# One written order for four engines up to the first values, a logarithm norm of x, and first weights loaded in quarters

## The chip, the cores and the metric

The kernel runs on one core of one Trainium2 chip. The metric is the device time of one execution in microseconds (us), lower is better. The median of three runs of the kernel before is 1539.29 us (1538.88 to 1541.18). One further execution was taken with the hardware profiler; its own time is 1536.77 us, and its span, from the first to the last instruction, 1535.1 us.

## The reference

Two layers of an encoder, 512 tokens by 1024 features, all in f32. The change touches only the head of layer 0: the first RMS norm and the products that take its result.

```python
def rms_norm(x, gain):
    xf = x.astype(jnp.float32)
    y = xf * lax.rsqrt(jnp.mean(xf * xf, axis=-1, keepdims=True) + EPS)
    return (y * gain.astype(jnp.float32)).astype(x.dtype)

def hgrn2_mixer(x, w_in, o_norm, w_out, lb):      # x is rms_norm(h, pre_mix_norm[0])
    proj = x @ w_in                                # 1024 -> 5 * 1024
    q, f_fw, f_bw, inp, gate = jnp.split(proj, ...)
    v = heads(inp)                                 # the "values"
    ...                                            # gated linear recurrence, both directions
    return (o * jax.nn.silu(gate)) @ w_out

def rope_angles(positions, dim):                   # needed only in layer 1
    inv = 1.0 / (ROPE_BASE ** (jnp.arange(0, dim, 2, dtype=jnp.float32) / dim))
    ang = positions.astype(jnp.float32)[..., None] * inv
    return jnp.cos(ang), jnp.sin(ang)

for i in range(DEPTH):
    a = rms_norm(h, pre_mix_norm[i])
    m = hgrn2_mixer(a, ...) if i % 2 == 0 else mla_mixer(a, positions, ...)
    h = h + rms_norm(m, post_mix_norm[i])
    f = squared_relu_mlp(rms_norm(h, pre_mlp_norm[i]), w_mlp_in[i], w_mlp_out[i])
    h = h + rms_norm(f, post_mlp_norm[i])
    h = h + rms_norm(jax.nn.sigmoid(h @ w_ple_gate[i]) * (p[i] @ w_ple_proj[i]), ple_norm[i])
```

## The kernel before

Every large product runs as three matmuls: each operand is split into a rounded part `hi` (type fp32r) and a rest `lo`, and hi·hi, hi·lo and lo·hi are summed in PSUM (`mm3`). A product's weights arrive by DMA in a raw tile (2048 columns, two buffers). The class `Weights` holds a written list of jobs; for each, ScalarE (ACT) makes `whi` by a copy to fp32r (L109) and VectorE (DVE) makes `wlo` by a subtraction. In the traces and orders below these are the tiles `whi`, `wlo` and `raw`.

Activations lie transposed: features on the 128 partitions, tokens on columns. So at the start x (four blocks of 128 tokens, tiles `x`, t = 0 to 3) is normed by row, transposed on TensorE (PE) in 128 by 128 pieces, and split with its gain into `ah` (ACT, L346) and `al` (DVE, L347); one `ah` tile holds two of the eight feature blocks k. `normed(ts)` does that for a list of token blocks: sum of squares, `rsqrt` (an integer guess and refinement in a dozen tiny DVE instructions), the scaling of x (L525), the transposes, the splits.

`first_values` multiplies the normed blocks with the first half of the value weights (four jobs "v", two raw tiles). Its results gather in the PSUM tiles `nm` (t=0), `sm` (t=1) and two `mm` tiles (t=2, 3): 24 matmuls of 512 columns for each t, 96 in all. After them comes the loop over the heads, which begins with the projections f, b, q and g of head 0, 24 matmuls each.

In the source the lower bound `lb` of the gates (tiles `mx`, `es`, `tot`) and the tables of the rotary angles come after that. The angles are a chain of small instructions on GpSimd (POOL), from the positions (`pos`, `posf`) through 15 rounds of `k`, `ang` (L577 to L586); then ACT takes a sine, an absolute value and a sine again (`sin_t`, `ang`, `cos_t`, L590 to L593). These need another table of functions than the rest of the kernel, so a table load stands ahead of them and one behind. Nothing reads `sin_t` and `cos_t` before layer 1. When they are done, the pool `start`, with x in it, is given back, and its memory is filled with x again (tile `H`, L602).

What sets the order: all loads of weights and of x are issued by SyncE (SP), in program order, on one DMA queue. On the computing engines the framework's scheduler lays the order down when the program is built, from a timeline of its own. Each engine then takes its instructions strictly in that order. Where the kernel wants its own order it wraps an engine in `Ordered` and calls `keep(True)`: instructions issued through the wrapper are then tied to each other in the order of the source. Before the change the head ties only PE's warm-up transposes.

Of the kernel before, what the change touches and what calls it, by code (L numbers as in the profile page):

```python
# [26 lines left out]
ALU = mybir.AluOpType  # L27
# [27 lines left out]
class Weights:  # L55

    def __init__(self, nc, pool, lo, ahead, raw_bufs, split_bufs):
        self.nc, self.pool, self.lo, self.ahead = nc, pool, lo, ahead  # L60
# [35 lines left out]
    def _split(self, i):  # L96
        nc = self.nc
        while self.n_split <= i and self.n_split < len(self.jobs):
            key, raw, lo_eng, copies, prep = self.jobs[self.n_split]
            if self.raws[raw][2] not in self.kinds:  # L100
                return
            self._load(raw)
            t = self.raws[raw][1][0]
            if prep:
                prep(t)
            hi = self.pool.tile([P, 1024], F32R, tag="whi", bufs=self.split_bufs, name=f"whi{self.n_split}")
            lo = self.pool.tile([P, 1024], F32R, tag="wlo", bufs=self.split_bufs, name=f"wlo{self.n_split}")
            for dst, src in copies:
                nc.scalar.copy(dst(hi), src(t))  # L109
# [26 lines left out]
class Ordered:  # L136


    def __init__(self, tc, eng):
        self.tc, self.eng, self.on, self.last = tc, eng, False, None  # L140

    def keep(self, on):
        self.on, self.last = on, None

    def __getattr__(self, name):
        def issue(*args, **kw):
            i = getattr(self.eng, name)(*args, **kw)  # L147
            if self.on:
                if self.last is not None:
                    self.tc.add_manual_dep(i.ins, self.last.ins.name, mybir.DependencyInfo(  # L150
                        mybir.DependencyClass.NoSync, mybir.DependencyReason.DATA), reason="in order")
                self.last = i
# [9 lines left out]
def trunk(  # L162
# [27 lines left out]
    def mm_tile():  # L190
        return T(pm, [P, S], "mm", 5)
# [5 lines left out]
        return T(pm, [P, S], "nm", 1)  # L197


    W = Weights(nc, wp, VN, ahead=4, raw_bufs=2, split_bufs=5)  # L200

    def plan_pair(keys, src, r0, c0, c1, lo=None):

# [286 lines left out]
    nc.sync.dma_start(pos, positions.rearrange("o (t p) -> p (o t)", p=P))  # L490
    nc.sync.dma_start(frq, freq.to_broadcast([P, 32]))

    warm = mm_tile()
    gps = mm_tile()
    PE.keep(True)
# [4 lines left out]
    PE.keep(False)  # L500
    V.tensor_copy(gains, gps[:, :ROWS])

    act = act_tiles()[0]
    ss, rx = T(sp, [P, NT], "ss"), T(sp, [P, NT], "rx")

    def normed(ts):

        a, n = ts[0], len(ts)
        hf = slice(a * P, (a + n) * P)
        for t in ts:  # L510
            v = ss[:, t : t + 1]
            if t < 3:
                junk = T(sp, [P, D], "junk", 2)
                A.activation(junk, xt[t], AF.Square, accum_out=v)
                V.tensor_scalar(v, v, 1.0 / D, EPS, op0=ALU.mult, op1=ALU.add)
            else:
                st, mv = T(sp, [P, 2, 6], "bn_st", 2), T(sp, [P, 2], "bn_mv", 2)
                for c in range(2):
                    V.bn_stats(st[:, c], xt[t][:, c * S : c * S + S])
                V.bn_aggr(mv, st)  # L520
                V.scalar_tensor_tensor(v, mv[:, 0:1], mv[:, 0:1], mv[:, 1:2], op0=ALU.mult, op1=ALU.add)
                V.tensor_scalar(v, v, EPS, None, op0=ALU.add)
        rsqrt(ss[:, a : a + n], rx[:, a : a + n])
        for t in ts:
            V.tensor_scalar(xt[t], xt[t], rx[:, t : t + 1], None, op0=ALU.mult)  # L525
        m = 2
        for k in range(0, NB, m):
            ps = mm_tile()
            for j in range(m):
                for t in range(n):  # L530
                    c = (n * j + t) * P
                    PE.transpose(ps[:, c : c + P], xt[a + t][:, (k + j) * P : (k + j + 1) * P], ident)
            for j in range(m):
                hi, lo = act[k + j]
                split(ps[:, j * n * P : (j + 1) * n * P], hi[:, hf], lo[:, hf], gain("pre_mix", k + j))
# [976 lines left out]
```

## Time and profile before

| | us |
|---|---|
| median of three runs | 1539.29 |
| the profiled execution | 1536.77 |
| its span | 1535.1 |
| PE busy in the span | 1499.4 (98%) |
| DVE busy | 1016.4 (66%) |
| ACT busy | 771.4 (50%) |
| POOL busy | 188.6 (12%) |
| mean granted clock of TensorE, share of full speed | 0.996 |

Times of rows count from the first instruction. "Busy" is the time in which an engine has an instruction under way; matmuls overlap, so a busy PE may still be slowed by its clock. A row of a timeline gives start, duration, engine, line and operation, and in brackets how long the engine had been idle and what ended that.

### The profile page before, as it was taken

Reading aid. Unit: us, or ns where it says so; the run is one execution under the profiler, and the core shown is the slowest. Engines: PE = TensorE matmul, PEld = TensorE weight load, DVE = VectorE, ACT = ScalarE, POOL = GpSimd, SP = SyncE. Lnnn points to the kernel's source line nnn. Section 1 sums busy time; section 2 is a strip of 40 time slices with the busy share of each in tenths; the row PEclk is TensorE's granted clock in tenths of the full one; section 3 lists DMA queues with packets and bytes.
Section 4 is the critical chain, followed back from the end, with each engine's and each line's share of the span. In section 5 each row is a group of like instructions: output and inputs, shape, how many; then the busy total and the mean of one; then the engine's idle time right before and its main releaser. Section 6 shows DMA issues by size and latency. Waiting matters only on the chain.

```text
span 1535.1 us, 19274 instructions
## 1 busy us (share of the span) xinstructions
PE 1499.4 (98%) x7379; PEld 1252.5 (82%) x7379; DVE 1016.4 (66%) x1842; ACT 771.4 (50%) x1319; POOL 188.6 (12%) x208
## 2 busy tenths in 40 slices
PE   8999999999999999999999999999999999999997
PEld 6888888889888787888887888888788887878885
DVE  6688578655675949456787784378464747677476
ACT  6555455356555454434645564466355645445332
POOL 4233132200000000000113331432000000000000
PEclk9999999999999999999999999999999999999999
DMA  5622332137151322314321111220552150604221
GB/s 168 204 57 82 83 83 83 42 121 245 47 178 42 141 79 75 117 57 136 118 88 30 42 56 56 59 81 30 185 186 82 36 184 1 220 0 137 85 81 55
DMA packets 109950, 147.86 MB, mean 96 GB/s; under 512 B 4781, under 2 KB 78114, under 8 KB 109602
## 3 DMA queue, kind: packets, MB, share of 16 engines
q1 hardware_dynamic: 109282, 145.58, 29.0%
q8 instruction: 58, 0.95, 0.3%
q10 hardware_dynamic: 576, 1.05, 0.2%
q14 instruction: 34, 0.28, 0.1%
HBM read 138.23 MB, written 8.39 MB: 96 GB/s over the span
## 4 chain that ended last, share of the span: by engine, by line
PE 86%; DVE 9%; ACT 3%; issue 1%; DMA 0%; POOL 0%; SPq 0%; DVEq 0%; ACTq 0%; POOLq 0%
PE mm L147 80%; PE sm L147 5%; DVE wlo L147 2%; PE nm L147 1%; ACT whi L109 1%; DVE ol L345 1%; DVE r L267 1%; DMA raw<-in_hg_w_in 0%; ACT ah L346 0%; DVE F L894 0%; ACT junk L861 0%; DVE rq_t L147 0%; DVE rope_d L1290 0%; DVE rope_d L1291 0%; DVE mx L1384 0%
## 5 line engine op out<-in xcount | busy, mean ns | idle before, releaser
L147 PE MATMUL mm<-ah,whi 128*128 128x512 f32 (+1 forms) x912 | 332.8, 370 | 2.5 <-ACT e L1002 1.0
L147 PE MATMUL mm<-ah,wlo 128*128 128x512 f32 (+1 forms) x912 | 329.8, 369 | 0.0
L147 PE MATMUL mm<-al,whi 128*128 128x512 f32 (+1 forms) x912 | 318.1, 368 | 0.0
L109 ACT CAST whi<-raw 128x1024 fp32r<-128x1024 f32 (+3 forms) x195 | 196.8, 1016 | 224.0 <-PE mm L147 184.0
L147 DVE TENSOR_TENSOR wlo<-raw,whi 128x1024 fp32r<-128x1024 f32 x165 | 207.7, 1269 | 147.3 <-ACT whi L109 146.5
L147 PEld LDWEIGHTS mm<-ah,whi 128*128 128x128 f32 x912 | 172.0, 189 | 31.6 <-ACT whi L109 2.6
L147 PEld LDWEIGHTS mm<-ah,wlo 128*128 128x128 f32 x912 | 172.0, 189 | 27.6
L147 PEld LDWEIGHTS mm<-al,whi 128*128 128x128 f32 x912 | 164.3, 189 | 27.2
L147 PE MATMUL mm<-wlo,oh 128*128 128x512 f32 x400 | 156.2, 390 | 4.0 <-DVE wlo L147 4.0
L147 PE MATMUL mm<-whi,ol 128*128 128x512 f32 x400 | 154.8, 389 | 0.0
L147 DVE TENSOR_TENSOR wlo<-r,whi 128x1024 fp32r<-128x1024 f32 x84 | 102.1, 1221 | 79.2 <-ACT whi L109 79.2
L147 PE MATMUL mm<-whi,oh 128*128 128x512 f32 x400 | 151.3, 391 | 0.7 <-DVE F L1045 0.7
L109 ACT CAST whi<-r 128x1024 fp32r<-128x1024 f32 x84 | 87.3, 1050 | 89.2 <-PE mm L147 89.2
L147 PE MATMUL mm<-whi,ah 128*128 128x512 f32 x304 | 119.2, 393 | 0.3 <-ACT ah L346 0.3
L147 PE MATMUL mm<-whi,al 128*128 128x512 f32 x304 | 118.6, 392 | 0.6 <-DVE al L345 0.6
L147 PE MATMUL mm<-wlo,ah 128*128 128x512 f32 x304 | 118.6, 390 | 0.0
L112 POOL TENSOR_TENSOR wlo<-raw,whi 128x512 fp32r<-128x512 f32 (+2 forms) x40 | 38.2, 981 | 560.3 <-ACT whi L109 553.3
L147 PEld LDWEIGHTS mm<-wlo,oh 128*128 128x128 f32 x400 | 75.1, 188 | 21.0 <-DVE wlo L147 5.7
L147 PEld LDWEIGHTS mm<-whi,oh 128*128 128x128 f32 x400 | 75.1, 188 | 16.4 <-DVE F L1045 1.1
L147 PEld LDWEIGHTS mm<-whi,ol 128*128 128x128 f32 x400 | 75.1, 188 | 15.6
L344 ACT CAST oh<-Z 128x512 fp32r<-128x512 f32 x84 | 51.5, 620 | 43.7 <-PE mm L147 42.6
L147 PEld LDWEIGHTS mm<-whi,al 128*128 128x128 f32 x304 | 57.1, 188 | 13.6 <-DVE al L345 1.9
(331 smaller groups left out, 2702.3 us busy)
## 6 DMA issues: line engine op xcount, KB each, us to landing
raw<-in_w_mlp_in SPq DMA_DIRECT2D x32, 1024.0 KB, 5.7
r<-in_w_mlp_out SPq DMA_DIRECT2D x24, 1024.0 KB, 9.5
raw<-in_hg_w_in SPq DMA_DIRECT2D x32, 512.0 KB, 5.3
raw<-in_w_mlp_out SPq DMA_DIRECT2D x8, 1024.0 KB, 5.1
raw<-in_w_ple_gate SPq DMA_DIRECT2D x8, 1024.0 KB, 5.2
raw<-in_mla_w_o SPq DMA_DIRECT2D x8, 1024.0 KB, 5.1
raw<-in_mla_w_uq SPq DMA_DIRECT2D x8, 576.0 KB, 4.1
raw<-in_hg_w_in SPq DMA_DIRECT2D x4, 1024.0 KB, 6.2
```

The source lines that it names most:

```text
L109: nc.scalar.copy(dst(hi), src(t))
L112: lo_eng.tensor_sub(dst(lo)[:, a], src(t)[:, a], f(dst(hi))[:, a])
L147: i = getattr(self.eng, name)(*args, **kw)
L267: nc.vector.tensor_sub(quad(t, *u), quad(t, *u), quad(t, *v))
L344: A.copy(hi, src)
L345: return V.tensor_sub(lo, src, f(hi))
```

## The change

`Ordered` gets a shared memory of the last instruction, so that two wrappers of one engine (`V` and `VN`, both VectorE) make one chain, and `A` (ScalarE) becomes ordered too. From the first instruction after the loads to the last of the first values, ACT, DVE and PE keep the order of the source. POOL keeps its own; `lb`, the angles, the sines and their table loads are issued after `keep(False)` and are placed between the ordered ones by the scheduler.

The norm of x takes a square on ACT for all four blocks, a logarithm and an exponential on ACT, and one Newton step on DVE in place of `rsqrt`. Blocks 0 and 1 are no longer scaled: the diagonal of 1/rms (`by`) takes the place of the identity in the transposing matmuls. Blocks 2 and 3 are scaled and transposed as before, with their splits and matmuls taking turns by pairs of k. The first weights come as four DMAs of 512 KB, two of them ahead of block 1 of x. There are 38 warm-up transposes in place of 30.

```diff
-    def __init__(self, tc, eng):
-        self.tc, self.eng, self.on, self.last = tc, eng, False, None
+    def __init__(self, tc, eng, mem=None):
+        self.tc, self.eng, self.on, self.mem = tc, eng, False, mem or [None]
...
-    A, G = nc.scalar, nc.gpsimd
-    V, PE = nc.vector, Ordered(tc, nc.tensor)
-
-    VN = Ordered(tc, nc.vector)
+    G = nc.gpsimd
+    A, V, PE = (Ordered(tc, e) for e in (nc.scalar, nc.vector, nc.tensor))
+
+    VN = Ordered(tc, nc.vector, V.mem)
...
-            r = W.raw([(lambda t: cols(t, 4, 512),
-                              hg_in[q * 512 : q * 512 + 512, 3072 + half * 512 : 3584 + half * 512]
-                              .rearrange("(k p) n -> p k n", p=P))])
+            r = W.raw([(lambda t, a=a: cols(t, 4, 512)[:, a : a + 2],
+                        hg_in[q * 512 + a * P : q * 512 + a * P + 256, 3072 + half * 512 : 3584 + half * 512]
+                        .rearrange("(k p) n -> p k n", p=P)) for a in (0, 2)])
...
+    W.prefetch(0)
     load(1)
     W.prefetch(1)
...
+    for e in (A, V, VN, PE):
+        e.keep(True)
...
-    for n in range(30):
+    for n in range(38):
         PE.transpose(warm[:, :P], ident, ident)
...
+    def norm(ts):
+        sl = slice(ts[0], ts[-1] + 1)
+        A.activation(rx[:, sl], ss[:, sl], AF.Ln, scale=1.0 / D, bias=eps)
+        V.tensor_scalar(rh[:, sl], ss[:, sl], -0.5 / D, -0.5 * EPS, op0=ALU.mult, op1=ALU.add)
+        A.activation(rx[:, sl], rx[:, sl], AF.Exp, scale=-0.5)
+        for t in ts:
+            c = slice(t, t + 1)
+            V.scalar_tensor_tensor(rt[:, c], rx[:, c], rh[:, c], rx[:, c], op0=ALU.mult, op1=ALU.mult)
+        V.scalar_tensor_tensor(rx[:, sl], rt[:, sl], 1.5, rx[:, sl], op0=ALU.add, op1=ALU.mult)
...
-    normed((0,))
-    first_values((0,), range(4))
-    normed((1,))
-    first_values((0,), range(4, NB))
-    first_values((1,), range(NB))
-    normed((2, 3))
+    squares(0)
+    norm((0,))
+    go, take0 = turned_by(0)
+    weights()
+    go()
+    take0((0, 1))
+    squares(1)
+    norm((1,))
+    go, take1 = turned_by(1)
+    take0((2, 3))
+    weights()
+    first_values((0,), (0, 1))
+    go()
+    first_values((0,), (2, 3))
+    take1(range(4))
+    first_values((1,), range(4))
+    for n in (2, 3):
+        ks = (2 * n, 2 * n + 1)
+        weights()
+        take0(ks)
+        take1(ks)
+        squares(n)
+        first_values((0,), ks)
+        first_values((1,), ks)
+    norm((2, 3))
+    for t in (2, 3):
+        V.tensor_scalar(xt[t], xt[t], rx[:, t : t + 1], None, op0=ALU.mult)
     psv += [mm_tile(), mm_tile()]
-    first_values((2, 3), range(NB))
+    hf = slice(2 * P, 4 * P)
+    for k in range(0, NB, 2):
...
+        for j in range(2):
+            split(ps[:, j * 256 : j * 256 + 256], act[k + j][0][:, hf], act[k + j][1][:, hf], gain("pre_mix", k + j))
+        if k >= 2:
+            first_values((2, 3), (k - 2, k - 1))
+        if k == 4:
+            W.hold([], 1)
+    first_values((2, 3), (NB - 2, NB - 1))
+    for e in (A, V, VN, PE):
+        e.keep(False)
```

The built order of ScalarE before the change, from the copy of the second value block (`v<-sm`) on: `ah<-mm` 128x256 are the splits of token blocks 2 and 3.

```order
L799 COPY v_77_537<-sm_155 128x512
L346 ACTIVATE ah_19_144<-mm_365,gains_82 128x256
L346 ACTIVATE ah_21_146<-mm_374,gains_82 128x256
L346 ACTIVATE ah_23_148<-mm_383,gains_82 128x256
L346 ACTIVATE ah_25_150<-mm_392,gains_82 128x256
L346 ACTIVATE ah_19_144<-mm_365,gains_82 128x256
L346 ACTIVATE ah_21_146<-mm_374,gains_82 128x256
L346 ACTIVATE ah_23_148<-mm_383,gains_82 128x256
L346 ACTIVATE ah_25_150<-mm_392,gains_82 128x256
L590 ACT_TABLE_LOAD
L590 ACTIVATE sin_t_86<-ang_469 128x128
```

The same place on ScalarE after the change; `rx` 128x2 are the logarithm and the exponential of blocks 2 and 3. (Wrapped instructions all carry the wrapper's line L147.)

```order
L147 ACTIVATE rx_165<-ss_164,eps_112 128x2
L147 COPY v_65_505<-sm_169 128x512
L147 ACTIVATE rx_165<-rx_165 128x2
L147 ACT_TABLE_LOAD
L147 ACTIVATE sin_t_86<-ang_437 128x128
L147 ACTIVATE ang_437<-ang_437 128x128
L147 ACTIVATE cos_t_87<-ang_437,half_pi_479 128x128
L147 ACT_TABLE_LOAD
L147 ACTIVATE ah_20_156<-mm_324,gains_82 128x256 x2
L147 ACTIVATE ah_22_158<-mm_333,gains_82 128x256 x2
L147 ACTIVATE ah_24_160<-mm_354,gains_82 128x256 x2
```

The two table loads and the three instructions on the angles stood behind the eight splits of blocks 2 and 3; now they stand ahead of all of them.

ScalarE from the last exponential of the lower bound on, before the change: `whi<-raw` are weight copies, `ah<-mm` 128x128 splits of token blocks 0 and 1, `junk` sums of squares.

```order
L567 ACTIVATE es_66_455<-es_66_455 128x8
L109 CAST whi_201<-raw_100 128x1024
L109 CAST whi_205<-raw_100 128x1024
L346 ACTIVATE ah_19_144<-mm_173,gains_82 128x128
L346 ACTIVATE ah_21_146<-mm_180,gains_82 128x128
L346 ACTIVATE ah_23_148<-mm_187,gains_82 128x128
L346 ACTIVATE ah_25_150<-mm_194,gains_82 128x128
```

The same place after the change.

```order
L147 CAST whi_181<-raw_99 128x1024
L147 ACTIVATE es_52_421<-es_52_421 128x8
L147 ACTIVATE es_53_422<-es_53_422 128x8
L147 ACTIVATE es_54_423<-es_54_423 128x8
L147 ACTIVATE ah_20_156<-mm_179,gains_82 128x128 x2
L147 ACTIVATE junk_197,ss_164<-x_11_92 128x1024
L147 ACTIVATE rx_165<-ss_164,eps_112 128x1
L147 ACTIVATE rx_165<-rx_165 128x1
L147 ACTIVATE ah_22_158<-mm_179,gains_82 128x128 x2
L147 CAST whi_212<-raw_99 128x1024
```

Where four splits went to four different tiles one after the other, they now come in pairs that write one tile, with one weight copy ahead of each second pair; in the built program the second split of a pair waits until DVE has made the `al` of the first. From the second projection of head 0 on, the order of PE is that of before.

## Rows read from the trace of the kernel before

**Rows 1.** Busy time of TensorE, from the page.

```profile
PE 1499.4 (98%) x7379; PEld 1252.5 (82%) x7379; DVE 1016.4 (66%) x1842; ACT 771.4 (50%) x1319; POOL 188.6 (12%) x208
```

**Rows 2.** Stretches: length, busy per engine, then granted clock, DMA share, GB/s.

```profile
8.90:16.90 8.00, 5.31 (x18) 2.69 (x18) 7.96 (x21) 7.49 (x16) 1.85 (x2) 0.78 1.00 340
16.90:20.10 3.20, 3.12 (x7) 2.48 (x8) 3.20 (x9) 1.07 (x2) 2.68 (x7) 0.50 1.06 279
...
42.00:64.00 22.00, 22.00 (x99) 18.22 (x98) 12.93 (x27) 11.45 (x20) 4.27 (x3) 1.00 0.71 203
```

**Rows 3.** Timeline of PE: start, duration, instruction.

```profile
30.02 0.47 PE L147 MATMUL mm<-whi,ah 128*128 128x512 f32 x1
...
41.90 0.39 PE L147 MATMUL mm<-ah,whi 128*128 128x512 f32 x1
...
47.34 0.39 PE L147 MATMUL mm<-ah,whi 128*128 128x512 f32 x1
```

**Rows 4.** Timeline of ACT from the second value copy to the second table load.

```profile
28.56 0.59 ACT L799 COPY v<-sm 128x512 f32<-128x512 f32 x1 [3.73 <-PE sm L147]
29.32 3.03 ACT L346 ACTIVATE ah<-mm,gains 128x256 fp32r<-128x256 f32 x8 [0.18 <-PE mm L147]
...
34.83 0.31 ACT L590 ACTIVATE sin_t<-ang 128x128 f32<-128x128 f32 x1 [1.17 <-POOL ang L586]
35.04 1.04 ACT L109 CAST whi<-raw 128x1024 fp32r<-128x1024 f32 x1
35.98 0.31 ACT L592 ACTIVATE ang<-ang 128x128 f32<-128x128 f32 x1
36.32 0.40 ACT L593 ACTIVATE cos_t<-ang,half_pi 128x128 f32<-128x128 f32 x1
36.74 1.28 ACT L463 ACT_TABLE_LOAD   x1
38.03 1.05 ACT L109 CAST whi<-raw 128x1024 fp32r<-128x1024 f32 x1
```

**Rows 5.** Timeline of POOL: first, two inner and last instruction of the angles.

```profile
14.97 1.56 POOL L577 CAST posf<-pos 128x4 f32<-128x4 int32 x1 [11.89 <-DMA pos<-in_positions]
...
18.26 0.46 POOL L586 TENSOR_TENSOR ang<-ang,k 128x128 f32<-128x128 f32 x1
...
19.18 1.30 POOL L586 TENSOR_TENSOR ang<-ang,k 128x128 f32<-128x128 f32 x1
...
34.33 0.46 POOL L586 TENSOR_TENSOR ang<-ang,k 128x128 f32<-128x128 f32 x1
```

**Rows 6.** Timeline of the start: warm-up, scaling of block 0, first weight copies.

```profile
5.12 2.69 PE L147 MATMUL mm<-ident 128*128 128x128 f32 x17
...
8.14 0.74 DVE L525 TENSOR_SCALAR x<-x,rx 128x1024 f32<-128x1024 f32 x1
...
9.41 1.99 ACT L109 CAST whi<-raw 128x1024 fp32r<-128x1024 f32 x2 [1.59 <-DMA raw<-in_hg_w_in]
```

**Rows 7.** Groups by form, first 60 us: count, busy us, mean ns, idle before.

```profile
L109 ACT CAST whi<-raw 128x1024 fp32r<-128x1024 f32 x12 | 12.4, 1050 | 7.9 <-DMA raw<-in_hg_w_in 7.5 <-PE mm L147 0.3
L346 ACT ACTIVATE ah<-mm,gains 128x128 fp32r<-128x128 f32 x16 | 4.9, 379 | 3.9 <-PE mm L147 3.8
L514 ACT ACTIVATE junk<-x 128x1024 f32<-128x1024 f32 x3 | 3.2, 1067 | 3.1 <-DMA x<-in_x 3.1
L147 DVE TENSOR_TENSOR wlo<-raw,whi 128x1024 fp32r<-128x1024 f32 x11 | 13.3, 1224 | 14.0 <-ACT whi L109 13.9
L347 DVE SCALAR_TENSOR_TENSOR al<-mm,gains,ah 128x128 fp32r<-128x128 f32 x16 | 4.9, 345 | 1.7 <-ACT ah L346 1.6
L525 DVE TENSOR_SCALAR x<-x,rx 128x1024 f32<-128x1024 f32 x4 | 3.3, 834 | 0.1
```

**Rows 8.** The reload of x (SP) and the first copy behind it (ACT).

```profile
36.79 0.37 SPq L602 DMA_DIRECT2D H<-in_x  x1
...
48.33 1.05 ACT L109 CAST whi<-raw 128x1024 fp32r<-128x1024 f32 x1 [5.64 <-DMA raw<-in_hg_w_in]
```

More of the change, by code (lines that the diff above doesn't have):

```diff
@@ L55, with __init__ @@
 class Weights:
-    def __init__(self, nc, pool, lo, ahead, raw_bufs, split_bufs):
-        self.nc, self.pool, self.lo, self.ahead = nc, pool, lo, ahead
+    def __init__(self, nc, pool, hi, lo, ahead, raw_bufs, split_bufs):
+        self.nc, self.pool, self.hi, self.lo, self.ahead = nc, pool, hi, lo, ahead
         self.split_bufs = split_bufs
@@ L108, in _split @@
             for dst, src in copies:
-                nc.scalar.copy(dst(hi), src(t))
+                self.hi.copy(dst(hi), src(t))
                 n = src(t).shape[1]
@@ L136 @@
 class Ordered:
-    def __init__(self, tc, eng):
-        self.tc, self.eng, self.on, self.last = tc, eng, False, None
+    def __init__(self, tc, eng, mem=None):
+        self.tc, self.eng, self.on, self.mem = tc, eng, False, mem or [None]
     def keep(self, on):
-        self.on, self.last = on, None
+        self.on, self.mem[0] = on, None
     def __getattr__(self, name):
@@ L148, in issue @@
             if self.on:
-                if self.last is not None:
-                    self.tc.add_manual_dep(i.ins, self.last.ins.name, mybir.DependencyInfo(
+                if self.mem[0] is not None:
+                    self.tc.add_manual_dep(i.ins, self.mem[0].ins.name, mybir.DependencyInfo(
                         mybir.DependencyClass.NoSync, mybir.DependencyReason.DATA), reason="in order")
-                self.last = i
+                self.mem[0] = i
             return i
@@ L197, in nm_bank @@
         return T(pm, [P, S], "nm", 1)
-    W = Weights(nc, wp, VN, ahead=4, raw_bufs=2, split_bufs=5)
+    W = Weights(nc, wp, A, VN, ahead=4, raw_bufs=2, split_bufs=5)
     def plan_pair(keys, src, r0, c0, c1, lo=None):
@@ L491, in trunk @@
     nc.sync.dma_start(frq, freq.to_broadcast([P, 32]))
+    for e in (A, V, VN, PE):
+        e.keep(True)
+    eps = T(sp, [P, 16], "eps")[:, :1]
+    V.memset(eps, EPS)
     warm = mm_tile()
     gps = mm_tile()
-    PE.keep(True)
-    for n in range(30):
+    for n in range(38):
         PE.transpose(warm[:, :P], ident, ident)
@@ L499, in trunk @@
             PE.transpose(gps[:, :P], graw, ident)
-    PE.keep(False)
     V.tensor_copy(gains, gps[:, :ROWS])
     act = act_tiles()[0]
[L504 to L509, printed above, removed]
-        for t in ts:
[L511 to L535, printed above, removed]
@@ new lines, in trunk, with squares @@
+    ss, rx, rh, rt = (T(sp, [P, NT], n) for n in ("ss", "rx", "rh", "rt"))
+    def squares(t):
+        A.activation(T(sp, [P, D], "junk", 2), xt[t], AF.Square, accum_out=ss[:, t : t + 1])
+    def norm(ts):
[3 more added lines that the diff above has]
+        A.activation(rx[:, sl], rx[:, sl], AF.Exp, scale=-0.5)
+        for t in ts:
+            c = slice(t, t + 1)
+            V.scalar_tensor_tensor(rt[:, c], rx[:, c], rh[:, c], rx[:, c], op0=ALU.mult, op1=ALU.mult)
+        V.scalar_tensor_tensor(rx[:, sl], rt[:, sl], 1.5, rx[:, sl], op0=ALU.add, op1=ALU.mult)
@@ new lines, in turned_by, with go, take @@
+    def turned_by(t):
+        by = T(sp, [P, P], f"by{t}")
+        V.tensor_scalar(by, ident, rx[:, t : t + 1], None, op0=ALU.mult)
+        pss = [mm_tile(), mm_tile()]
+        def go():
+            for k in range(NB):
+                PE.matmul(pss[k // 4][:, k % 4 * P : k % 4 * P + P], lhsT=xt[t][:, k * P : k * P + P], rhs=by,
+                          start=True, stop=True)
+        def take(ks):
+            for k in ks:
+                sl = slice(t * P, t * P + P)
+                split(pss[k // 4][:, k % 4 * P : k % 4 * P + P], act[k][0][:, sl], act[k][1][:, sl], gain("pre_mix", k))
+        return go, take
@@ L538, in trunk, with weights @@
     wv, psv = [], [nm_bank(), sm_tile()]
+    def weights():
+        wv.append(W.hold([("v", 0, len(wv))], 0)[0])
     def first_values(ts, ks):
         for k in ks:
-            if k // 2 == len(wv):
-                wv.append(W.next(("v", 0, k // 2)))
             wh, wl = (cols(t, 2, 512)[:, k % 2] for t in wv[k // 2])
@@ L547, in first_values @@
                 mm3(psv[t], act[k][0][:, sl], act[k][1][:, sl], wh, wl, k == 0, k == NB - 1)
-    normed((0,))
-    first_values((0,), range(4))
-    normed((1,))
-    first_values((0,), range(4, NB))
-    first_values((1,), range(NB))
-    normed((2, 3))
-    psv += [mm_tile(), mm_tile()]
-    first_values((2, 3), range(NB))
+    squares(0)
[25 more added lines that the diff above has]
+        V.tensor_scalar(xt[t], xt[t], rx[:, t : t + 1], None, op0=ALU.mult)
+    psv += [mm_tile(), mm_tile()]
+    hf = slice(2 * P, 4 * P)
+    for k in range(0, NB, 2):
+        ps = mm_tile()
+        for c in range(4):
+            PE.transpose(ps[:, c * P : c * P + P], xt[2 + c % 2][:, (k + c // 2) * P : (k + c // 2) * P + P], ident)
+        for j in range(2):
[7 more added lines that the diff above has]
+        e.keep(False)
     show("a0", [f(a[0]) for a in act])
```

## The prediction

> **What bounds the kernel now.** I read the page first: TensorE (PE) is busy 98% of the span [rows 1]. Then busy time and granted clock by stretches [rows 2]: from 42 us on PE is full at the upper of its two clock levels, and only ahead of that is there anything to win. There PE is part idle (5.31 of 8.0 us busy from 8.9 to 16.9) and runs at 0.50, 1.2 GHz, until about 20. Then the timeline of PE [rows 3]: the first matmul on values of blocks 2 and 3 starts at 30.02 us, projection f of head 0 at 41.90, projection b at 47.34. From there PE is the bound to the end, so what the head of the kernel gains or loses before b's start goes one to one into the time. I forecast the start of b.
>
> **The wait that moves.** The timeline of ACT [rows 4] shows the three instructions on the rotary angles. The sine starts at 34.83, after 1.17 us in which ACT waited for POOL; in before that wait is free, because all eight splits of blocks 2 and 3 (29.32 on) are through by then. In the built order of after, sine, absolute value, second sine and both table loads stand ahead of all eight splits. An engine takes its instructions in order, so no split of blocks 2 and 3 can begin until POOL has finished the angles and ACT has done these.
>
> When does POOL finish? Its chain runs from the landing of `pos` at 14.97 to 34.33 + 0.46 = 34.79 [rows 5]. The change adds nothing to POOL and takes nothing from it, and `pos` stays behind the same bytes on SP's one queue (four blocks of x, 2 MB of weights, the gains). I take 34.79 again.
>
> Then sine from 34.83, 0.31; absolute value 0.31; second sine 0.40; table load 1.28 [rows 4]: 34.83 + 2.30 = 37.13 (the weight copy that lay between them in before is elsewhere now; the first table load lies in the wait). The first split and its way to PE take 0.70 in before (29.32 to 30.02), of which some belongs to the transposes; I take 0.5. First matmul on blocks 2 and 3: 37.6 in place of 30.02, **+7.6 us**.
>
> From there to the start of b, before took 47.34 - 30.02 = 17.3 us for 72 matmuls, which at the distance of full clock (47.34 - 41.90 = 5.44 for 24, so 0.227 each) are 16.3; 1.0 was waiting for splits. After has the same 72, no such wait, since a pair of k costs PE 12 × 0.227 = 2.7 us and ACT and DVE less, but 8 of the 16 transposes now lie between them, about 0.1 us each. **0**.
>
> **The clock.** PE's work on blocks 0 and 1 ends at about 28 to 29 us (below); until 37.6 it has only some transposes, against 5.31 busy of 8.0 us in the stretch in which the clock fell in before. There the lower level then lasted 3.2 us into dense work (16.9 to 20.1) [rows 2]. The same at 37.6 would cost half of 3.2, **+1.5 us**. If the clock stays up it costs nothing; I take 1.5, since PE will have been much idler than where the row shows the fall.
>
> **What else the change does, and why it weighs little.** All of it lies ahead of the wait, so it counts only if it makes the chain longer than 37.1 us.
> - Norm of block 0. The sum of squares is there at about the same time. In before DVE had scaled x by 8.14 + 0.74 = 8.9 us [rows 6]; logarithm, exponential and Newton step drop some ten DVE instructions and the scaling. But 38 warm-up transposes take PE, which keeps its order, from 7.81 (5.12 + 2.69) to 7.81 + 8 × 0.158 = 9.1 (2.69/17 = 0.158 each). The transposes of block 0 start at 9.1, as before: no gain. Whatever the two new tiny ACT instructions cost is covered there, with over a microsecond to spare.
> - Quarters of weights. The first copy waited for 1 MB until 9.41 [rows 6]; now half a megabyte lands where block 1 of x did, and copy and rest are done by about 8.7. The first value matmul starts near 10.1. Block 1 of x comes 3 us later, but its square stands behind two splits anyway.
> - The pairs. Before, the splits went four in a row to different tiles; now the second of a pair waits for DVE's `al` of the first. From 9.4 ACT has [rows 4, 7]: 16 splits × 0.38 = 6.1; three sums of squares × 1.25 (1.07 and the read of the sum) = 3.7; three weight copies × 1.05 = 3.1; four small ones, 0.8; two value copies × 0.59 = 1.2: together 15.0. To that come eight waits for an `al` × 0.345 = 2.8, and three times DVE first makes a `wlo`, 1.22 each = 3.7. So the last exponential ends at 9.4 + 15.0 + 2.8 + 3.7 = 30.9, PE's last matmul on block 1 shortly before, and with the two scalings of x (0.83 each), the Newton step and the first transposes blocks 2 and 3 are ready to split at about 33.5. That is 4 us later than in before (29.3), and still ahead of 37.1.
> - The sums of squares of block 3 move from DVE to ACT; counted. The later value loads come as 512 KB pieces too: two more issues on SP, beside a queue that is ahead of its readers: nothing.
> - What is late next. The reload of x (`H`) needs the last transposes of blocks 2 and 3, which go from 30 to about 45 us, so it is issued some 8 us later than 36.79, and head 1's weights stand behind it. In before their copy ran at 48.33 [rows 8], so now near 57; PE needs them after 96 matmuls of head 0, 21.8 us after the start of f (41.90 before, some 9 us later now, so at about 73). 15 us to spare: 0.
>
> **The sum**, against the profiled execution's own 1536.77 us: +7.6 + 1.5 + 0 = 1545.9. The median of before is 2.5 us above that execution, so against the median 1548.4 us.
>
> **Bounds.** POOL's chain is 36 instructions of 0.3 to 0.46 us and a few stretched ones, as 1.30 beside 0.46 for the same form [rows 5]. Undisturbed and with `pos` a little earlier it might end 2.5 us sooner; with two more stretched ones 1.7 later. The clock costs 0 to 1.5. Together +5.1 to +10.8.
>
> Two rules of the Trainium skill speak on this term; the sum goes by the rows. "ScalarE: Activation LUTs", section What ACT_TABLE_LOAD costs, says a switch of table costs 1283 ns and a drain of about 1380 ns more. The row has 1.28 us, and the next copy starts 0.01 us behind it [rows 4], so no such drain is seen here; by the page the sum would be an estimated 1549.8. "GPSIMD Engine Reference", section Specifications, says that GpSimd shares its interfaces to memory with VectorE, and collides with its instructions that have two inputs in SBUF. The 1.30 above may be that (DVE makes a `wlo` then), and after makes as many in POOL's time: one more hit would be 0.8, within the bounds above.
>
> **Rivals.**
> 1. POOL is in time and the pairs set the end. If POOL ended before about 31 (33.5 less 2.3), the first split would be at 33.5 and the first matmul at 34.0: +4.0, with the clock 0 to 1.5 more: 1543.3 to 1544.8. For it: the scheduler put the sine there, so by its own timeline POOL was done. Against it: 34.79 in the trace.
> 2. Faster. The written order feeds PE without a gap from 10.1 on: 48 matmuls × 0.227 and 16 transposes of some 0.11 end at 22.8, blocks 2 and 3 follow at 25 to 26, 4 to 5 us ahead of 30.02: 1534 to 1535. It decides only if POOL ends before 23, so with `pos` landing at about 3 us, and if ACT and DVE need far less than worked out. The head start of the quarters (the first copy starts near 6.5 in place of 9.41) speaks for it, POOL's chain [rows 5] against it.
> 3. The change does not do what it says: order and waits come out as before, gains and losses of the start cancel, 1536.5 to 1542.
>
> **How the numbers follow.** The wait for POOL has 0.67 (1544.4 to 1550.5), the pairs 0.16, no difference 0.10, faster 0.07. What a measurement of this kernel can tell from no change is about 0.2%, 3.1 us. Slower: 0.67 + 0.16 = 0.83; same 0.10; faster 0.07. The predicted time is that of the first case, 1548.4. The range takes in the first case, the pairs, and a microsecond for the median: 1542 to 1551.
>
> **What would show it.** In the trace after: ACT's sine starts right behind a wait of some 4 us for POOL's `ang`, at about 35; splits of blocks 2 and 3 at about 37; on PE a gap of several us ended by `ah`, then 3 us at a granted clock of 0.50; b's first matmul near 56.4. POOL's last `ang` before 31 would make rival 1 right, a first matmul on blocks 2 and 3 before 30 would make me wrong altogether, and so would a start of b at 56 with a total of before: then the loss is given back later.

## The result, and the profile after

The changed kernel takes 1552.83 us (median of 5 runs, 1550.74 to 1553.38); the kernel before took 1539.29. The ratio is 1.0084, 95% interval 1.0074 to 1.0095. It is slower, as forecast, and beyond the upper end of the range, 1551. The profiled execution took 1551.82 us, its span is 1550.1, against 1536.77 and 1535.1 before: 15.0 us more.

Busy time of the engines, from the page; it answers [rows 1]. PE is busy for 8.8 us more. Its work grew by 24 short instructions, eight warm-up transposes and sixteen in the products with `by` (they show as 32 where the transposes of blocks 0 and 1 were 16); most of the rest is the same work at a lower clock, as the stretches below show.

```profile
PE 1508.2 (97%) x7403; PEld 1260.8 (81%) x7403; DVE 1013.4 (65%) x1816; ACT 773.9 (50%) x1327; POOL 189.8 (12%) x208
```

The timeline of ACT where the order was changed (start, duration, instruction, and in brackets the idle time before it and who ended it); it answers [rows 4].

```profile
29.95 0.21 ACT L147 ACTIVATE rx<-rx 128x2 f32<-128x2 f32 x1
30.17 1.28 ACT L147 ACT_TABLE_LOAD   x1
35.16 0.31 ACT L147 ACTIVATE sin_t<-ang 128x128 f32<-128x128 f32 x1 [3.71 <-POOL ang L625]
35.50 0.31 ACT L147 ACTIVATE ang<-ang 128x128 f32<-128x128 f32 x1
35.85 0.40 ACT L147 ACTIVATE cos_t<-ang,half_pi 128x128 f32<-128x128 f32 x1
36.27 1.28 ACT L147 ACT_TABLE_LOAD   x1
37.56 0.47 ACT L147 ACTIVATE ah<-mm,gains 128x256 fp32r<-128x256 f32 x1
```

The sine waits 3.71 us for POOL, and every split of blocks 2 and 3 waits behind it: the first starts at 37.56, where before all eight were under way from 29.32. POOL's first and last instruction on the angles answer [rows 5]; it ends at 35.13, 0.34 later than before.

```profile
15.11 0.59 POOL L616 CAST posf<-pos 128x4 f32<-128x4 int32 x1 [12.04 <-DMA pos<-in_positions]
...
34.68 0.45 POOL L625 TENSOR_TENSOR ang<-ang,k 128x128 f32<-128x128 f32 x1
```

PE, whose rows answer [rows 3]: the transposes of blocks 2 and 3, the first matmul on their values (30.02 before), and a matmul of projection b that stood at 47.34 before.

```profile
31.88 0.30 PE L147 MATMUL mm<-ident,x 128*128 128x128 f32 x1 [2.45 <-DVE x L147]
32.65 1.28 PE L147 MATMUL mm<-ident,x 128*128 128x128 f32 x7 [0.47 <-DVE x L147]
38.09 0.79 PE L147 MATMUL mm<-whi,ah 128*128 128x512 f32 x1 [4.16 <-ACT ah L147]
...
57.97 0.39 PE L147 MATMUL mm<-al,whi 128*128 128x512 f32 x1
```

Then the stretches (from, to, length; busy time and instructions of PE, PE's weight loads, DVE, ACT, POOL; granted clock, DMA share, GB/s); they answer [rows 2].

```profile
33.40:43.40 10.00, 5.84 (x16) 4.17 (x15) 1.84 (x4) 4.09 (x8) 1.48 (x4) 0.50 0.00 0
43.40:60.00 16.60, 16.60 (x78) 13.80 (x77) 6.52 (x9) 7.89 (x12) 0.00 (x0) 1.00 0.73 231
290.00:296.00 6.00, 3.77 (x22) 2.94 (x21) 4.93 (x10) 2.03 (x5) 3.15 (x3) 1.00 0.44 169
296.00:299.40 3.40, 3.40 (x19) 3.40 (x18) 1.56 (x3) 0.72 (x4) 0.00 (x0) 0.50 0.00 0
...
814.80:818.30 3.50, 3.50 (x9) 2.73 (x9) 3.37 (x9) 1.23 (x2) 0.00 (x0) 0.51 0.54 169
825.10:828.50 3.40, 3.40 (x11) 2.62 (x10) 2.16 (x9) 2.47 (x8) 1.36 (x2) 0.50 0.00 0
```

PE's clock stands at 0.50 (1.2 GHz) for the whole wait and for 5.3 us of dense work behind it (38.09 to 43.4): the twelve matmuls there take 5.28 us instead of 12 × 0.227 = 2.72, so they cost 2.6 us more. (It is low from 26.4 to 29.8 too; that lies ahead of the wait for POOL and costs nothing.) Besides the last 5 to 8 us, where it is low in every trace, it falls three more times much later, each time when PE has been nearly idle for some 2 us (from 290 to 296, for one, it is busy for 3.77 us of 6). In the profiled execution of before PE nearly idles at the same places (from 808 to 811 it is busy for 0.98 us of 3.00), and the clock stays up:

```profile
285.00:288.00 3.00, 2.99 (x24) 2.67 (x23) 1.74 (x3) 1.66 (x11) 0.00 (x0) 1.00 0.00 0
...
802.50:806.00 3.50, 3.50 (x16) 2.63 (x16) 3.37 (x9) 1.24 (x2) 0.00 (x0) 1.00 0.56 169
808.00:811.00 3.00, 0.98 (x4) 0.67 (x4) 2.83 (x12) 1.69 (x5) 0.00 (x0) 1.00 0.00 0
811.00:814.00 3.00, 3.00 (x15) 2.38 (x14) 2.73 (x10) 2.98 (x8) 1.37 (x2) 1.00 0.00 0
```

If each matmul of after is laid beside the same matmul of before, the whole loss can be read as an offset: +10.6 us at 87 us and the same up to 285, +12.3 behind 288, +15.1 behind 813, and the same at the end. So 10.6 us are lost in the first 45 us, and 4.4 in the three later falls of the clock.

The reload of x and the first weight copy behind it answer [rows 8]; nothing waits for them.

```profile
47.34 0.37 SPq L641 DMA_DIRECT2D H<-in_x  x1
...
58.88 1.05 ACT L147 CAST whi<-raw 128x1024 fp32r<-128x1024 f32 x1
```

### The profile page after: what moved, and what is told of

Same layout as the page of the kernel before. It is cut to its first block, busy times and chain, and to the rows that moved or that the text cites. A ratio compares the mean times of both kernels' runs of the same rounds, so it can differ in the third digit from the quotient of the medians.

```text
span 1550.1 us, 19317 instructions
## 1 busy us (share of the span) xinstructions
PE 1508.2 (97%) x7403; PEld 1260.8 (81%) x7403; DVE 1013.4 (65%) x1816; ACT 773.9 (50%) x1327; POOL 189.8 (12%) x208
## 4 chain that ended last, share of the span: by engine, by line
PE 85%; DVE 9%; ACT 2%; POOL 1%; issue 1%; DMA 1%; SPq 0%; DVEq 0%; ACTq 0%; POOLq 0%
PE mm L147 80%; PE sm L147 5%; DVE wlo L147 2%; PE nm L147 1%; DVE ol L147 1%; DVE r L267 1%; DVE F L147 1%; DVE rope_d L147 1%; ACT whi L147 1%; DMA pos<-in_positions 1%; POOL ang L625 1%; ACT junk L147 0%; POOL k L624 0%; DVE rq_t L147 0%; DVE al L147 0%
## 5 line engine op out<-in xcount | busy, mean ns | idle before, releaser
L147 PE MATMUL mm<-ah,whi 128*128 128x512 f32 (+1 forms) x912 | 332.9, 370 | 2.3 <-ACT e L147 1.0
L147 PE MATMUL mm<-ah,wlo 128*128 128x512 f32 (+1 forms) x912 | 329.8, 369 | 0.0
L147 PE MATMUL mm<-al,whi 128*128 128x512 f32 (+1 forms) x912 | 318.4, 368 | 0.0
L147 ACT CAST whi<-raw 128x1024 fp32r<-128x1024 f32 (+3 forms) x195 | 196.8, 1016 | 215.0 <-PE mm L147 184.6
L147 DVE TENSOR_TENSOR wlo<-raw,whi 128x1024 fp32r<-128x1024 f32 x165 | 207.7, 1268 | 143.5 <-ACT whi L147 142.3
L147 PEld LDWEIGHTS mm<-ah,whi 128*128 128x128 f32 x912 | 172.2, 189 | 31.5 <-ACT whi L147 2.6
L147 PEld LDWEIGHTS mm<-ah,wlo 128*128 128x128 f32 x912 | 172.1, 189 | 27.6
L147 PEld LDWEIGHTS mm<-al,whi 128*128 128x128 f32 x912 | 164.4, 189 | 27.0
L147 PE MATMUL mm<-wlo,oh 128*128 128x512 f32 x400 | 156.3, 391 | 4.0 <-DVE wlo L147 4.0
L147 PE MATMUL mm<-whi,ol 128*128 128x512 f32 x400 | 154.9, 390 | 0.0
L147 DVE TENSOR_TENSOR wlo<-r,whi 128x1024 fp32r<-128x1024 f32 x84 | 102.0, 1220 | 80.9 <-ACT whi L147 80.9
L147 PE MATMUL mm<-whi,oh 128*128 128x512 f32 x400 | 151.6, 392 | 0.7 <-DVE F L147 0.7
L147 ACT CAST whi<-r 128x1024 fp32r<-128x1024 f32 x84 | 87.3, 1051 | 90.7 <-PE mm L147 90.7
L147 PE MATMUL mm<-whi,ah 128*128 128x512 f32 x304 | 120.4, 397 | 4.2 <-ACT ah L147 4.2
L147 PE MATMUL mm<-whi,al 128*128 128x512 f32 x304 | 120.0, 395 | 0.6 <-DVE al L147 0.6
L147 PE MATMUL mm<-wlo,ah 128*128 128x512 f32 x304 | 119.6, 394 | 0.0
L147 PEld LDWEIGHTS mm<-wlo,oh 128*128 128x128 f32 x400 | 75.2, 188 | 21.0 <-DVE wlo L147 5.7
L147 PEld LDWEIGHTS mm<-whi,oh 128*128 128x128 f32 x400 | 75.3, 188 | 16.4 <-DVE F L147 1.1
L147 PEld LDWEIGHTS mm<-whi,ol 128*128 128x128 f32 x400 | 75.1, 188 | 15.6
L147 ACT CAST oh<-Z 128x512 fp32r<-128x512 f32 x84 | 51.5, 620 | 43.8 <-PE mm L147 42.7
L147 PEld LDWEIGHTS mm<-whi,ah 128*128 128x128 f32 x304 | 57.7, 190 | 15.9 <-ACT ah L147 4.6
```

## The experiments

Theory: the sines ahead of the splits make PE wait for POOL, and that is the loss. Rivals: the new chain of paired splits is as late by itself; the idle PE's clock is most of it; what is lost later belongs to the new order too.

**The sine behind the last split, the rest as changed.**

```diff
+    last_split = A.mem[0]                  # behind the last take of blocks 2, 3
...
-    A.activation(sin_t, ang, AF.Sin)
+    first_sine = A.activation(sin_t, ang, AF.Sin)
+    tc.add_manual_dep(first_sine.ins, last_split.ins.name, ...)
```

> The changed kernel, with one more tie: the first sine may not stand on ScalarE before the last split of blocks 2 and 3. If the wait for POOL's angles is what holds the first matmul on blocks 2 and 3 at 38.1 us, it now starts at about 33.3, when the transposes are there, and the total falls by 4.8 us and by what the lower clock then costs less (0 to 2.6): 1545 to 1548 against 1552.8. If the paired splits alone set that start, nothing changes (1552 to 1553). If the later stretches of lower clock belong to the changed order of the head, they stay; if they depend on where the program happens to stand, they may go.

1543.89 us; ratio to before 1.0028 (1.0017 to 1.0040). Two thirds of the loss are back, 8.9 us of 13.5, more than expected. ACT and PE of this run: the first split waits for PE's transposes now, and the sine, far behind, for nobody. Of the three later falls of the clock two are still there.

```profile
33.77 0.47 ACT L147 ACTIVATE ah<-mm,gains 128x256 fp32r<-128x256 f32 x1 [3.01 <-PE mm L147]
...
47.52 0.31 ACT L147 ACTIVATE sin_t<-ang 128x128 f32<-128x128 f32 x1
```

```profile
34.30 0.80 PE L147 MATMUL mm<-whi,ah 128*128 128x512 f32 x1
```

**The other way round: before, with only the sines and both table loads ahead of the eight splits.**

```diff
-    normed((2, 3))
+    normed((2, 3), sines)      # sines(): Sin, Abs, Sin, table load; ACT kept in order to the last split
```

> The kernel before, with only this moved: the sines and both table loads stand on ScalarE ahead of the eight splits of blocks 2 and 3, which keep their order (all first halves, then all second halves). If the place of the sine is the cause, this alone moves the first matmul on blocks 2 and 3 from 30.0 to about 37.7 us and costs 7.6 us plus 0 to 2.6 for the clock: 1547 to 1549.5 against 1539.3. If the loss needs the rest of the change, it costs at most 2 us.

1548.79 us, with before at 1540.10 beside it; ratio 1.0059 (1.0046 to 1.0071), as the theory had it. ACT and PE: the same picture as in the changed kernel, with POOL 1.2 us later in this execution, PE waiting for 9.21 us, and the clock at half until 44.5.

```profile
36.35 0.31 ACT L147 ACTIVATE sin_t<-ang 128x128 f32<-128x128 f32 x1 [6.12 <-POOL ang L577]
...
38.75 3.04 ACT L147 ACTIVATE ah<-mm,gains 128x256 fp32r<-128x256 f32 x8
```

```profile
39.28 0.79 PE L147 MATMUL mm<-whi,ah 128*128 128x512 f32 x1 [9.21 <-ACT ah L147]
```

So this one edit costs 8.7 us alone and gives 8.9 back when undone.

**PE kept at work in the wait (the changed kernel, with idle transposes).**

```diff
+    fill = mm_tile()
+    def busy(n):
+        for _ in range(n):
+            PE.transpose(fill[:, :P], ident, ident)
+    busy(18)                   # ahead of the transposes of blocks 2, 3
...
+        if k == 2:
+            busy(28)           # ahead of the first values of blocks 2, 3
```

> The changed kernel, with 18 idle transposes on TensorE ahead of the transposes of blocks 2 and 3 and 28 behind the first eight, where TensorE waits anyway. If the granted clock fell because TensorE waited there, it stays up, the first twelve matmuls take 2.7 us in place of 5.3, and the total falls by 2.6: about 1550.2. If the clock has no part in it: no change, 1552.8.

1550.69 us; ratio 1.0070 (1.0057 to 1.0082). The first matmuls on blocks 2 and 3 come at full clock (0.50 and 0.39 us, not 0.79); a stretch of half clock follows, but is shorter.

```profile
29.36 2.13 PE L147 MATMUL mm<-ident 128*128 128x128 f32 x18
33.44 3.22 PE L147 MATMUL mm<-ident 128*128 128x128 f32 x28
39.53 0.50 PE L147 MATMUL mm<-whi,ah 128*128 128x512 f32 x1 [2.86 <-ACT ah L147]
39.87 0.39 PE L147 MATMUL mm<-wlo,ah 128*128 128x512 f32 x1
```

```profile
40.40:43.80 3.40, 3.40 (x10) 2.66 (x9) 1.36 (x3) 0.94 (x3) 0.00 (x0) 0.51 0.00 0
```

By the medians the clock in the wait is worth some 2 us of the loss, not most of it. The intervals of the two kernels overlap, and in the one trace of this run, with POOL at its end only at 36.6, what is lost between this first matmul and projection b is 1.7 us instead of 2.6.

**POOL's input first: the changed kernel, `pos` and `frq` loaded ahead of the weights.**

```diff
+    nc.sync.dma_start(pos, ...)            # both now behind the gains' load,
+    nc.sync.dma_start(frq, ...)            # ahead of the first weights and x's blocks 1 to 3
     W.prefetch(0)
```

(A tie keeps the sine where the change has it.)

> The changed kernel, with the loads of positions and frequencies (18 KB) issued ahead of the first weights, and the sine kept behind the last exponential of the norm, where it stands in the changed kernel too. POOL then ends its angles some 8 us earlier, and ScalarE does sines and table loads between the norm and the splits without a wait. If waiting for POOL is the cause, the first matmul on blocks 2 and 3 starts at about 34.4 and the total is 3.7 to 6 us lower: 1547 to 1549. If what costs is the place of the table loads and not the wait: no gain, 1552 to 1553.

1550.58 us; ratio 1.0070 (1.0056 to 1.0083): 2.2 us won where 3.7 to 6 were expected. POOL is done at 27.3, and ACT waits no more, but the first matmul on blocks 2 and 3 stands at 37.01, not at 34.4:

```profile
32.56 0.22 ACT L147 ACTIVATE rx<-rx 128x2 f32<-128x2 f32 x1
32.80 1.28 ACT L147 ACT_TABLE_LOAD   x1
34.09 0.31 ACT L147 ACTIVATE sin_t<-ang 128x128 f32<-128x128 f32 x1
```

```profile
37.01 0.80 PE L147 MATMUL mm<-whi,ah 128*128 128x512 f32 x1 [0.58 <-ACT ah L147]
```

The last exponential is at 32.56 instead of 29.95, and table loads and sines (3.7 us) still stand between it and the splits. So neither the wait alone nor the place of the table loads alone fits this run. The early loads cost the others: from 4.5 to 7.0 us, first this run, then the changed kernel,

```profile
4.50:7.00 2.50, 2.20 (x12) 1.99 (x11) 1.03 (x9) 1.65 (x4) 0.19 (x1) 1.00 0.70 139
```

```profile
4.50:7.00 2.50, 2.43 (x18) 2.23 (x17) 1.31 (x10) 2.44 (x5) 0.00 (x0) 1.00 1.02 342
```

139 GB/s instead of 342. `pos` is 2 KB in pieces of 4 bytes; that it and the replicated `frq` are what slows the queue is argued from these rates, not isolated. Not all of it is theirs: other executions of the changed order were at 262 to 324 GB/s there, with the first weight copy at 7.4 to 8.2 where the changed kernel's first trace has 6.07 and this run 9.40.

**Both kernels again, for a second trace.**

> The kernel before, unchanged, for a second trace of it. Theory: its time lies between 1537.7 and 1541.2 us like its other executions, the first matmul on values of blocks 2 and 3 stands near 30 us again, and where the time is above 1538 the granted clock falls to 0.50 for some 3.4 us at one or more of the three places at which TensorE nearly idles for 2 us (near 282, 800 and 810 us). Rival: such falls belong to the changed kernel alone, and what differs between executions of before lies in its first 50 us.

> The changed kernel, unchanged, for a second trace and more times. Theory: 1550 to 1554 us; the sine again starts behind POOL's last angle (33 to 37 us) and the first matmul on blocks 2 and 3 follows 2.9 to 3.0 us behind the sine; against before the offset of the head is 10 to 12 us in its trace, and what is left of the difference is 0 to 4.4 us of later falls of the clock, other in number than the three of the first trace. Rival: the three later falls belong to this order of instructions and come again at the same places in every trace.

Before: 1537.7 us, one run, no later fall of the clock, the head 0.9 later than in the first trace. After: 1552.47 us; ratio 1.0083 (1.0070 to 1.0097). POOL ended at 36.4, the first matmul on blocks 2 and 3 stood at 39.40 and the offset of the head was 11.5. The three later falls came again, 4.3 us in all, so my expectation that their number would differ was wrong. Yet they aren't after's alone: of 23 runs of before on one chip the fastest, 1535.7 us, had a mean granted clock of 0.998, the five slowest, 1541.4 to 1541.8, of 0.992: 18 us more at half clock, for some 6 us of time. None of these runs was traced, so where their clock fell isn't seen. The five traces taken of before and of its variants have no later fall (one of them with the waits of PE filled, below). All seven of the changed kernel and its variants with those waits unfilled have some: both of the changed kernel, that with PE kept at work and that with POOL's input first have three, the sine behind and the untied pairs (below) two, the untied pairs with the sines ahead one.

**The pairs untied (and the sine behind).** In each pair of splits both of ACT's parts now stand ahead of DVE's.

```diff
+    def splits(jobs):
+        for src, hi, lo, scale in jobs:
+            A.activation(hi, src, AF.Copy, scale=scale)
+        for src, hi, lo, scale in jobs:
+            V.scalar_tensor_tensor(lo, src, scale, f(hi), op0=ALU.mult, op1=ALU.subtract)
...
-            for k in ks: ... split(...)
+            splits([(...) for k in ks])
```

> The changed kernel with its sine behind the last split, and in each pair of splits both of ACT's parts stand ahead of both of VectorE's, so ACT waits for VectorE once a pair and not in the middle of it. Theory (the pairs carry what is left of the loss): the last exponential of the norm comes 2 to 3 us sooner than in the kernel with the sine behind alone, the first matmul on blocks 2 and 3 at 31.5 to 32.5, and the time is 1541 to 1542.5 us. Rival (the rest of the loss lies in the wait for x and weights or in the later clock): 1543.3 to 1545 us, as without this edit.

1534.84 us; ratio to before 0.9969 (0.9959 to 0.9979): faster than before, and 9 us better than with the pairs tied, where I expected 1.4 to 2.9. The split's group on ACT from 8 to 31 us (count, busy, mean ns, idle before it), first in the changed kernel, then untied:

```profile
L147 ACT ACTIVATE ah<-mm,gains 128x128 fp32r<-128x128 f32 x16 | 5.6, 365 | 8.6 <-DVE al L147 6.8 <-PE mm L147 1.9
```

```profile
L147 ACT ACTIVATE ah<-mm,gains 128x128 fp32r<-128x128 f32 x16 | 4.7, 386 | 0.6 <-PE mm L147 0.6
```

6.8 us of waits for `al` are gone (they held more than the one `al` each: DVE's `wlo` stands between). The norm of blocks 2 and 3 and PE follow:

```profile
21.81 0.20 ACT L147 ACTIVATE rx<-rx 128x2 f32<-128x2 f32 x1
...
25.33 1.57 ACT L147 ACTIVATE ah<-mm,gains 128x256 fp32r<-128x256 f32 x4
```

```profile
25.86 0.50 PE L147 MATMUL mm<-whi,ah 128*128 128x512 f32 x1
```

The first matmul on blocks 2 and 3 is 4.2 us ahead of before's, and PE's clock does not fall in the whole head. Which parts of the change (norm, order, `by`) make this kernel faster than before isn't told apart.

**The pairs untied, but the sines ahead as the change has them.**

```diff
+    A.activation(sin_t, ang, AF.Sin)       # Sin, Abs, Sin and the table load ahead of
+    ...                                    # the loop over the splits of blocks 2, 3
```

> The pairs untied as before, but the two sines, the absolute value and both table loads ahead of all eight splits of blocks 2 and 3, as the change has them. Theory (the pairs cost nothing as long as ACT waits for POOL behind them): the norm's last exponential stands near 22 us, the sine waits from there to POOL's last angle (35 to 37.5 us), the first matmul on blocks 2 and 3 comes at 38 to 40.5 us, and the time is 1550 to 1554 us, as if the pairs had not been touched; TensorE is then idle for longer, 24 to 38 us. Rival (the two costs add up): 9 us less than the changed kernel, 1542 to 1545 us.

1547.98 us; ratio 1.0061 (1.0048 to 1.0075).

```profile
25.38 1.28 ACT L147 ACT_TABLE_LOAD   x1
35.24 0.31 ACT L147 ACTIVATE sin_t<-ang 128x128 f32<-128x128 f32 x1 [8.57 <-POOL ang L600]
...
37.64 1.57 ACT L147 ACTIVATE ah<-mm,gains 128x256 fp32r<-128x256 f32 x4
```

```profile
38.16 0.80 PE L147 MATMUL mm<-whi,ah 128*128 128x512 f32 x1 [12.46 <-ACT ah L147]
```

ACT is there 4.8 us sooner and waits that much longer; PE starts at 38.16, as with the pairs tied (38.09). So behind the wait for POOL the pairs are free, and the costs do not add. The time is 2 us below what I expected, and the trace has three reasons for that: POOL ended at 35.2, as in the changed kernel's first trace, where in three others of the changed order it ended at 36.3 to 36.6; half clock lasted until 41.7 only; and one later fall was there, not three. With the pairs untied the place of the sine costs 1547.98 - 1534.84 = 13.1 us, where it cost 8.7 and 8.9 above: its price depends on how early the splits could start without it.

**The later waits of PE filled, in three kernels.** Twice 16 idle transposes, ahead of the first scores of layer 1's heads 0 and 1 (near 800 and 810 us).

```diff
+        if h == 1:
+            idle(sm_tile(), 16)
...
             ps = mm_tile()
+            if h == 0 and t == 0:
+                idle(ps, 16)               # 16 transposes of ident
```

> The kernel before, with 2 x 16 idle transposes on TensorE in the two waits near 800 and 810 us (ahead of the first scores of heads 0 and 1 of the second layer). Theory (the falls of the clock behind these waits are what spreads its executions from 1536 to 1541.8 us): no half clock near 800 to 820 us in any trace, spread at most 2.5 us, median 1537 to 1538.5 us. Rival (the falls come from elsewhere, or the transposes cost what they save): median 1539 to 1541 us, spread as before.

> The changed kernel, with the same 2 x 16 idle transposes at the same two places. Theory (two of the three later falls gone, 2.9 us in its first trace): 1549 to 1550.5 us, and the profile shows full clock from 800 to 840 us. Rival (what the changed kernel loses beyond its first 50 us is no matter of the clock): 1551.5 to 1553.5 us.

> The kernel with the sine behind the last split and the pairs untied, with the same idle transposes. Theory: 1532.5 to 1534 us, 1 to 2 us below the same kernel without them. Rival: 1534 to 1535.5 us.

Before 1537.35 (ratio 0.9983, 0.9975 to 0.9992; spread 2.5 us instead of 4 to 6); the changed kernel 1549.46 (1.0060, 1.0047 to 1.0072); untied 1533.00 (0.9952, 0.9939 to 0.9964), the fastest of all. Each gains 1.8 to 3.4 us, all three within what the theory gave. The mean granted clock of before's runs is 0.995 to 0.998 with the waits filled and 0.992 to 0.996 without, so before's own untraced runs did lose time at these two places. Stretch of both waits in the changed kernel, second trace, without and with them:

```profile
796.00:830.00 34.00, 30.04 (x132) 23.96 (x131) 30.00 (x78) 15.36 (x30) 5.70 (x6) 0.90 0.19 60
```

```profile
796.00:830.00 34.00, 32.98 (x179) 27.70 (x178) 31.21 (x82) 15.94 (x31) 5.87 (x6) 1.00 0.20 63
```

**The quarters alone, on before.**

```diff
-            r = W.raw([(lambda t: cols(t, 4, 512), hg_in[q * 512 : q * 512 + 512, ...])])
+            r = W.raw([(lambda t, a=a: cols(t, 4, 512)[:, a : a + 2], hg_in[...]) for a in (0, 2)])
...
+    W.prefetch(0)
     load(1)
```

> The kernel before with one part of the change alone: the first weights loaded in pieces of 512 KB, the first half of them ahead of block 1 of x. Theory (as the prediction had it): the first weight copy starts 1 to 3 us sooner than 9.4, block 1 of x comes later but its square stands behind other work, and the time stays within 1538 to 1541 us. Rival: block 1 of x is late, the second norm with it, and the time rises by 1 to 3 us, to 1541 to 1543 us.

1540.73 us; ratio 1.0012 (1.0003 to 1.0021). The first weight copy starts at 8.08 (9.41 and 10.36 in before's two traces), block 1 of x is squared at 10.73 instead of 7.59 in the second. No gain; whether the small loss is block 1's delay or the order that the scheduler then chose is not told apart.

## Why the prediction was off

**The wait that moves** was right. Forecast: first split 37.13, first matmul on blocks 2 and 3 at 37.6, +7.6. Measured: 37.56 and 38.09, +8.1; 0.34 of the difference is POOL, which was taken at 34.79 and ended at 35.13 (35.2 to 36.6 in other executions with the sines ahead in the changed order; the prediction's bound of 1.7 reached 36.5). Done alone and undone alone, this edit is worth 8.7 and 8.9 us.

**The clock term (+1.5)** was right in kind and too small. The prediction carried over the 3.2 us at half clock of before's first gap. After the longer wait half clock covered 5.3 us of dense work and cost 2.6, above the 0 to 1.5 that the bounds had allowed. Keeping PE busy in the wait won 2.1 by the medians. (By the prediction's own terms, +10.8, the upper end of its first case is 1550.1, not 1550.5.)

**The 72 matmuls behind it (0)**: right. 8.1 + 2.6 is the offset of 10.6 that the head has.

**The step that failed** is "what the head of the kernel gains or loses before b's start goes one to one into the time". Up to 285 us it does. Then PE's clock falls three times in after, 4.4 us in its trace, and in the profiled execution of before it doesn't. I had read [rows 2] up to 64 us and took it that PE is the bound at one speed from there; three waits of 2 us, at 282, 800 and 810 us, were in the trace and I didn't look for them. With two of them filled the changed kernel takes 1549.46 us, inside the range and 1.1 from the forecast, but before gains by the same filling. The Trainium skill, "TensorE: Matmul & The Clock Gate", Part 1, says that where the clock changes differs from run to run, because what watches PE's activity isn't started with the kernel. Before's runs agree, from 1535.7 us at a clock of 0.998 to 1541.8 at 0.992. All nine runs of after had a low clock (0.990 to 0.992), and its three falls came in both of its traces; why there, when before's runs vary so widely, stays open.

**The sum against the median.** Added to 1536.77, an execution without later falls, and then moved by 2.5 us to the median, the forecast held some of them already. By the medians the change costs 13.5 us, where the forecast had 9.1: 4.4 too few. With both later waits filled in both kernels it costs 1549.46 - 1537.35 = 12.1 us; in these two traces the head of after is 10.5 us behind, and the fall near 296 us, which is still there, takes most of the rest. So an estimated 1.5 of the missing 4.4 us lie in the head (0.5 in the wait, 1.1 in the clock), 1.6 in the fall near 296 us, and 1.4 in the falls at 800 and 810 us that after has more of than before. This division sets offsets of single traces beside medians, so it is a rough one.

**What weighed little.** The first value matmul stood at 9.90 (10.1 forecast), the last exponential at 29.95 (30.9), the transposes from 31.9 on (splits ready at 33.5). The waits for `al` in the pairs came to 6.8 us (2.8 + 3.7 forecast). H was issued 10.6 us later, not 8, and head 1's first copy at 58.88 is still well ahead of its use near 73: nothing, as costed. That the pairs weigh nothing behind the wait is shown by the kernel that unties them and keeps the sines: PE starts at 38.16.

**The rivals.** Rival 1 (POOL in time, the pairs set the end) is what the kernel with the sine behind shows: 34.30 for the forecast 34.0, and 1543.89 within its 1543.3 to 1544.8. Rival 2 (faster) is the untied kernel, with its first matmul at 25.86 for the forecast "25 to 26" and 1534.84 for 1534 to 1535. That it fits so well is in part luck, for its conditions were wrong: POOL need not end before 23 if the sine is behind (it ended at 38.0), and what stood in its way were the pairs, not the length of ACT's work.

**The two rules.** The next instruction starts 0.01 us behind the table load of 1.28 (36.27 to 37.56): the drain that "ScalarE: Activation LUTs" of the Trainium skill gives (What ACT_TABLE_LOAD costs) was again not there. "GPSIMD Engine Reference" of the Trainium skill, Specifications (POOL collides with VectorE's instructions that have two inputs in SBUF), fits better than forecast. In after POOL's two longest angle instructions start at 18.91 (1.34) and 23.88 (1.46), 0.05 and 0.08 us behind the start of a `wlo` on DVE. In the untied kernel DVE makes three `wlo` in a row, and POOL's instructions are stretched (0.30 and 0.46 when alone) for about as long; DVE first, then POOL:

```profile
31.60 3.85 DVE L147 TENSOR_TENSOR wlo<-raw,whi 128x1024 fp32r<-128x1024 f32 x3
```

```profile
31.12 0.46 POOL L632 TENSOR_TENSOR ang<-ang,k 128x128 f32<-128x128 f32 x1
31.67 1.31 POOL L631 TENSOR_SCALAR k<-kk 128x128 f32<-128x128 f32 x1
33.07 1.30 POOL L632 TENSOR_TENSOR ang<-ang,k 128x128 f32<-128x128 f32 x1
34.46 1.16 POOL L631 TENSOR_SCALAR k<-kk 128x128 f32<-128x128 f32 x1
35.70 0.46 POOL L632 TENSOR_TENSOR ang<-ang,k 128x128 f32<-128x128 f32 x1
```

POOL's instructions beside DVE's scaling of x, which reads one tensor only, are stretched too, if less (0.84 and 0.62 in after, at 31.20 and 32.13); the rule as the prediction gave it doesn't cover them. No run took DVE's work away to test it.

## What to carry to other kernels

If an engine's order is fixed by a scheduler's own clock, look what a waiting instruction holds up behind it on that engine: ACT's sine cost 9 us here, and 13 with the pairs untied, because it waited for a chain on POOL that no matmul there needed. Write the halves of a pair so that one engine does both of its parts before the other's turn: 9 us here, hidden until the sine was moved. And before carrying a gain "one to one" to the end, search the whole trace for idle gaps of PE: filled with idle transposes they gave 0.2%.

## What the runs showed that I had not expected

- Waits of PE of 2 us, near 800 and 810 us, cost 1.4 us each in clock in some executions and nothing in others; 2 x 16 idle transposes took this away and narrowed before's spread to 2.5 us.
- The first loads differ between executions of one order: the first weight copy of the changed kernel started at 6.07 and, in the second trace, 7.81 us.
- A POOL instruction that starts within a 1.2 us `wlo` of DVE lasts until that ends or a little longer (1.1 to 1.5 us). With that, and with `pos` landing at 15.0 to 16.5 us, POOL's angles ended between 34.8 and 38.0 us in kernels that did not touch them.
